# The first products of a hybrid decoder layer, issued kind by kind

## The chip, the cores and the metric

The kernel runs on one core of one Trainium2 chip. A time is device microseconds (us) for one execution of the whole layer. The profile is of one execution; its span goes from the first to the last instruction that the profiler saw.

Engines: PE (TensorE) multiplies matrices and has a weight-load stream of its own (PEld); DVE (VectorE) and ACT (ScalarE) do elementwise work; POOL (GpSimd) does little here; SP (SyncE) issues nearly all transfers. Each engine takes its instructions strictly in the order in which they were built; between engines they wait on semaphores.

## The reference, cut to what matters

```python
def hybrid_layer(x, norm1_w, w_in, ...):
    h = rmsnorm(x, norm1_w)
    proj = h @ w_in                       # ONE input projection, its columns split:
    qkv_a, z_a, b_a, a_a, qkv_b = ...     # gated DeltaNet (q, k, v, z, b, a) and attention
    qkv_a = silu(causal_dwconv(qkv_a, conv_qkv_w))
    ...                                   # L2-normed q and k, chunked delta rule, gated norm
    o_b = dilated_attention(qb, kb, vb)   # 3 dilated windows merged by their denominators
    x = x + concat([o_a, o_b]) @ w_out
    u = causal_dwconv(rmsnorm(x, norm2_w) @ w_up, ffn_conv_w)
    return x + (silu(gate) * up) @ w_down # and a final RMSNorm behind it
```

Sequence 1024, model width 1024, 4 DeltaNet heads of 128, 8 attention heads of 64, feed-forward width 2816, all float32.

## The kernel before, in words

Every large product is made of three. A float32 operand is split in a high part rounded to fp32r (`hi`) and the rest (`lo`); `mm3` (L204) adds w_hi·x_hi, w_hi·x_lo and w_lo·x_hi in one PSUM bank. The helper `split` (L210) makes `hi` with a copy on ACT and `lo` with a subtraction on DVE. `split_x` (L280) does the same for the input `xt`, times the norm's weight `n1`.

**The start.** The input comes as eight tiles `xt` of 128 rows (the contraction) by 1024 tokens, the weights of the keys of heads 0 to 2 as four tiles `wst` of two contraction tiles each (the loop over k at L300). Tile 0 comes in two halves of 512 tokens. `squares(k)` (L286) squares a tile on ACT and adds it to `acc` on DVE, for the RMSNorm, whose factor is applied only after the products. Meanwhile PE multiplies a tile of ones, `warm`, ten times (L355); a float32 product shows as two passes in the profile, so these are 20 rows.

**The first products.** `first` (L361) runs over the 8 contraction tiles; for each, over six PSUM banks `pst`, that is three heads times two halves of 512 tokens, with three products each: 144 products of 512 columns. The profile names them by what they read: `ps<-xhi,whi`, `ps<-xlo,whi`, `ps<-xhi,wlo`. A bank is complete with its last product at the eighth tile.

**What follows it.** `norms` (L380) slips small products in between: `ps<-xt,wba`, `ps<-acc,pick` (sums of squares), then `bat` and `rst` on DVE, a power on POOL, and two groups of four transposes of `rst` on PE, which DVE copies to `rstdB`. `gates` (L411) makes the decays `g` and their sums (`ps<-g,tri`). `first_keys` (L501) takes the six banks out: DVE multiplies each by `rstdB` (rows `xr<-ps,rstdB`), and `conv_silu` (L460) makes the keys `kT` of a head: one copy on ACT, three steps on DVE (`kT<-xr,gcw,kT` over 1023, 1022 and 1021 columns), a tanh on ACT (`xr<-kT`), a last step on DVE (`kT<-xr,kT`). `kprep` (L587) fills decay tiles `dec` on POOL with a select, exponentiates them on ACT, and transposes the keys on PE (`ps<-ident,kT`). `dense` (L508) then makes the other columns of the projection with 48 products each, in two banks that take turns with the first banks of `pst`.

**What sets the order.** Streams (`first`, `dense`, `norms`, `gates` and others) yield a time at which they may go on; `Weave` (L46) keeps a planned clock for PE and for each engine (`free`, `ready`) and lets the most urgent stream that is ready issue next. This fixes PE's order. DVE's and ACT's orders come from a scheduler that works on the finished program with a timeline of its own; `after` (L188) adds an order between two instructions without a wait.

Of the kernel before, what the change touches and what calls it, by code (L numbers as in the profile page):

```python
# [7 lines left out]
F32 = mybir.dt.float32  # L8
F32R = mybir.dt.float32r
AF = mybir.ActivationFunctionType  # L10
OP = mybir.AluOpType
# [4 lines left out]
P = 128  # L16
S = 1024
KT = 8
# [126 lines left out]
def hybrid_layer(tc, I, out):  # L145
    nc = tc.nc
    wv = Weave()
    ve = Engine(wv, nc.vector, "vector", 0.07, 0.00105)
    ac = Engine(wv, nc.scalar, "scalar", 0.12, 0.00085)

# [15 lines left out]
    def tile_(pool, shape, dt, name, tag, bufs):  # L166
        return wv.slot(pool.tile(list(shape), dt, name=name, tag=tag, bufs=bufs), tag, bufs)
# [3 lines left out]
    def A(name, tag, dt=F32, shape=(P, 1024)):  # L171
        if tag in TURNS:
            i = turns[tag] = turns.get(tag, -1) + 1
            tag = TURNS[tag][i % len(TURNS[tag])]
        return tile_(lp, shape, dt, name, tag, SLOTS[tag])

    def X(name, dt=F32R):
        return A(name, "X", dt)

    def const(name, shape, src=None):  # L180
        t = cp.tile(list(shape), F32, name=name)
        if src is not None:
            sy.dma_start(t, src)
        return t
# [3 lines left out]
    def after(inst, anchor, reason="keeps a slot free until it is needed"):  # L188
        tc.add_manual_dep(inst.ins, anchor.ins.name, order, reason=reason)

    def mm(dst, lhs, rhs, us, start=True, stop=True, **kw):
        tc.stamp_issue_order_token(nc.tensor.matmul(dst, lhs, rhs, start=start, stop=stop, **kw).ins, TOKEN)  # L192
        wv.product(us, dst, lhs, rhs)
# [10 lines left out]
    def mm3(dst, lhs, rhs, first, last, **kw):  # L204
        us = 0.2135 * rhs[0].shape[-1] / 512
        mm(dst, lhs[0], rhs[0], us, first, False, **kw)
        mm(dst, lhs[0], rhs[1], us, False, False, **kw)
        mm(dst, lhs[1], rhs[0], us, False, last, **kw)

    def split(src, hi, lo):  # L210
        ac.activation(hi, src, AF.Copy)
        return ve.tensor_tensor(lo, src, hi.bitcast(F32), op=OP.subtract)
# [19 lines left out]
    n1 = const("n1", [P, KT])  # L232
# [25 lines left out]
    def bank(tag, name="ps"):  # L258
        return tile_(pp_, (P, 512), F32, name, tag, 2)
# [7 lines left out]
    def half(i):  # L267
        return slice(i * 512, i * 512 + 512)
# [7 lines left out]
    xs, xts = [], []  # L276
# [3 lines left out]
    def split_x(xt, k, sl):  # L280
        hi, lo = xs[k]
        ac.activation(hi[:, sl], xt[:, sl], AF.Copy, scale=n1[:, k:k + 1])
        ve.scalar_tensor_tensor(lo[:, sl], xt[:, sl], n1[:, k:k + 1], hi[:, sl].bitcast(F32), op0=OP.mult,
                                op1=OP.subtract)

    def squares(k):  # L286

        sqs[k] = A("sq", "qa")
        ac.activation(sqs[k], xts[k], AF.Square)
        if k == 1:  # L290
            ve.tensor_tensor(acc, sqs[0], sqs[1], op=OP.add)
        elif k > 1:
            inst = ve.tensor_tensor(acc, acc, sqs[k], op=OP.add)
            if k == 6:
                after(inst, first_lo, "the products wait for these weights")
# [4 lines left out]
    for k in range(KT):  # L300
        if k == 4:

            sy.dma_start(wba[:, :, :8], I["wba"])
        xt = A("xt", ("kT*", "dv*")[k % 2])
        xts.append(xt)
        if k % 2 == 0:
            wst = tile_(wp, [P, 2, 384], F32, "wst", "wst", 2)
            whi, wlo = [A(nm, "uy", F32R, (P, 2, 384)) if k < 4 else A(nm, "kt", F32R, (P, 2, 384))
                        for nm in ("whi", "wlo")]
            wk0.append((whi, wlo))  # L310
        xs.append((X("xhi"), X("xlo")))
        if k == 0:
            sy.dma_start(wst[:, 0, :], I["w0"][0, :, 0])
            for h in range(2):
                sy.dma_start(xt[:, half(h)], I["xT"][:P, half(h)])
            sy.dma_start(wst[:, 1, :], I["w0"][0, :, 1])
            split(wst[:, 0, :], whi[:, 0, :], wlo[:, 0, :])
            for h in range(2):
                split_x(xt, 0, half(h))
            split(wst[:, 1, :], whi[:, 1, :], wlo[:, 1, :])  # L320
        else:
            if k % 2 == 0:
                sy.dma_start(wst, I["w0"][k // 2])
            parts = [half(0), half(1)] if k == 1 else [slice(0, S)]
            for sl in parts:
                sy.dma_start(xt[:, sl], I["xT"][k * P:(k + 1) * P, sl])
            if k % 2 == 0:
                wlast = split(wst, whi, wlo)
            for sl in parts:
                split_x(xt, k, sl)  # L330
            squares(k - 1)
        if k == 4:
            first_lo = wlast
        if k == 6:
            ve.tensor_tensor(wba[:, :, :8], wba[:, :, :8], n1[:, :, None].to_broadcast([P, KT, 8]), op=OP.mult)
    squares(KT - 1)


# [13 lines left out]
    ve.tensor_scalar(gw2, gnw, 0.5, None, op0=OP.mult)  # L352

    wbank = bank("atr", "warm")
    for _ in range(10):  # L355
        mm(wbank[:, :P], warm, warm, 0.3)


    pst = [bank(t) for t in ("hf", "asc", "ch") for _ in range(2)]

    def first():  # L361
        for k in range(KT):
            w = wk0[k // 2]
            for i in range(6) if k > 1 else (0, 2, 4, 1, 3, 5):
                yield wv.need(*xs[k], *w)
                m, h = divmod(i, 2)
                wm = [t[:, k % 2, m * P:(m + 1) * P] for t in w]
                mm3(pst[i], wm, [t[:, half(h)] for t in xs[k]], k == 0, k == KT - 1)
        wv.done.add("first")


# [1178 lines left out]
    def down(pd, i, op, sl, first, last_):  # L1550
        (whi, wlo), (hhi, hlo) = op
        c = slice(i * P, (i + 1) * P)
        mm3(pd[:, sl], (whi[:, c], wlo[:, c]), (hhi[:, sl], hlo[:, sl]), first, last_, skip_group_check=True)
# [229 lines left out]
```

## Time and profile before

| what | value |
|---|---|
| time, median of 3 runs | 1191.49 us (1191.37 to 1192.41) |
| time of the profiled execution | 1191.63 us |
| its span | 1189.8 us |
| PE busy | 1180.1 us, 99% of the span |
| DVE busy | 965.4 us, 81% |
| ACT busy | 573.2 us, 48% |
| POOL busy | 54.6 us, 5% |
| granted TensorE clock, mean | 0.998 |

A timeline row reads: start in us, length in us, engine, line of the kernel, operation, what it writes<-reads, shape, count; in brackets the engine's idle time before it and who ended it. Rows that follow each other with equal names are merged. The length of a matmul row holds its pipeline; the distance between two starts is what a product costs. Line 139 is the helper that records every DVE and ACT operation and line 192 is the one for products, so the names of the tiles tell what a row is.

### The profile page before, as it was taken

What the parts mean: (1) busy time and instruction counts of PE and PEld (TensorE: products, weight loads), DVE (VectorE), ACT (ScalarE), POOL (GpSimd) and SP (SyncE); (2) the same over time, 40 slices, a digit from 0 to 9 for tenths busy, and PEclk for the clock granted to TensorE, in tenths of its full rate; (3) what the DMA queues carried; (4) which work ended last, traced back from release to release, by engine and by line L of the source; (5) the groups of instructions that cost most, each with busy time, mean ns of one, the idle gap of its engine ahead of it and who ended that gap; (6) DMA issues with size and microseconds to landing.
All of it is one profiled execution on the core that took longest, in us unless ns stands there. A gap on an engine that the chain in (4) does not pass through costs nothing.

```text
span 1189.8 us, 18253 instructions
## 1 busy us (share of the span) xinstructions
PE 1180.1 (99%) x6994; PEld 975.9 (82%) x6994; DVE 965.4 (81%) x1545; ACT 573.2 (48%) x1122; POOL 54.6 (5%) x49
## 2 busy tenths in 40 slices
PE   9999999999999999999999999999999999999997
PEld 7888888888777777888888888888888888888887
DVE  7776996474677787677998898989889889898987
ACT  7473444363434444555554444545444553546452
POOL 0212001013000000000000000000000000000001
PEclk9999999999999999999999999999999999999999
DMA  7423457647552414343221313122231395356734
GB/s 239 107 94 84 114 144 163 201 149 186 166 147 72 99 37 151 142 159 107 89 92 68 107 53 107 57 103 81 80 102 58 120 377 202 124 178 220 239 98 160
DMA packets 114520, 156.91 MB, mean 132 GB/s; under 512 B 54368, under 2 KB 65408, under 8 KB 114432
## 3 DMA queue, kind: packets, MB, share of 16 engines
q1 hardware_dynamic: 113712, 155.21, 41.4%
q8 instruction: 55, 0.90, 0.3%
q10 hardware_dynamic: 720, 0.53, 0.1%
q14 instruction: 33, 0.27, 0.1%
HBM read 117.68 MB, written 38.03 MB: 131 GB/s over the span
## 4 chain that ended last, share of the span: by engine, by line
PE 97%; DVE 1%; ACT 0%; issue 0%; DVEq 0%; ACTq 0%
PE ps L192 47%; PE pa L192 20%; PE dw L192 18%; PE pc L192 10%; PE ps L201 1%; PE ps L196 1%; PE warm L192 0%; DVE x1h L139 0%; ACT sm L141 0%; DVE sm L141 0%; PE pd L192 0%; DVE avt L139 0%; DVE aqkv L139 0%; DVE wke L141 0%; DVE ct L141 0%
## 5 line engine op out<-in xcount | busy, mean ns | idle before, releaser
L192 PE MATMUL dw<-pr 128*128 128x512 f32 (+1 forms) x984 | 211.4, 376 | 0.0
L192 PEld LDWEIGHTS dw<-pr 128*128 128x128 f32 x984 | 176.7, 188 | 33.7
L192 PE MATMUL ps<-xhi,whi 128*128 128x512 f32 x448 | 183.7, 410 | 0.0
L192 PE MATMUL ps<-xhi,wlo 128*128 128x512 f32 x448 | 175.2, 391 | 0.0
L192 PE MATMUL ps<-xlo,whi 128*128 128x512 f32 x448 | 174.9, 391 | 0.0
L192 PE MATMUL pa<-T,pair 128*128 128x512 f32 x528 | 126.8, 389 | 0.0
L192 PEld LDWEIGHTS pa<-T,pair 128*128 128x128 f32 x528 | 99.1, 188 | 20.6
L192 PEld LDWEIGHTS ps<-xhi,whi 128*128 128x128 f32 x448 | 84.2, 188 | 18.9 <-issue 2.7
L192 PEld LDWEIGHTS ps<-xhi,wlo 128*128 128x128 f32 x448 | 84.1, 188 | 18.3
L192 PEld LDWEIGHTS ps<-xlo,whi 128*128 128x128 f32 x448 | 84.4, 188 | 14.9 <-DVE xlo L139 0.3
L139 ACT ACTIVATE u<-pa 128x512 f32<-128x512 f32 x44 | 26.4, 599 | 114.4 <-PE pa L192 114.4
L139 DVE SCALAR_TENSOR_TENSOR y<-xu,fcw,y 128x1023 f32<-128x1023 f32 (+1 forms) x44 | 56.4, 1281 | 22.1 <-ACT y L139 22.0
L139 ACT ACTIVATE pr<-wd 128x1024 fp32r<-128x1024 f32 x33 | 35.0, 1061 | 73.4 <-DVE wd L139 35.8
L192 PE MATMUL pa<-B,A 128*128 128x512 f32 x264 | 63.5, 389 | 0.0
L192 PE MATMUL pc<-B,pair 128*128 128x512 f32 x264 | 63.4, 389 | 0.0
L192 PE MATMUL pc<-T,S 128*128 128x512 f32 x264 | 63.4, 389 | 0.0
L192 PE MATMUL pa<-T,S 128*128 128x512 f32 x264 | 63.4, 389 | 0.0
L139 DVE TENSOR_TENSOR wst<-wst 128x512 f32<-128x512 f32 x88 | 60.4, 686 | 0.8
L139 ACT ACTIVATE whi<-wst 128x1024 fp32r<-128x1024 f32 (+2 forms) x38 | 38.5, 1013 | 46.5 <-PE ps L192 38.9
L192 PE MATMUL ps<-B,pair 128*128 128x512 f32 x252 | 60.5, 389 | 0.0
L141 ACT ACTIVATE sm<-sm,mx 128x128 f32<-128x128 f32 (+7 forms) x64 | 35.5, 556 | 49.7 <-DVE mx L141 49.7
L192 PEld LDWEIGHTS pa<-T,S 128*128 128x128 f32 x264 | 49.6, 188 | 10.3
(248 smaller groups left out, 2229.8 us busy)
## 6 DMA issues: line engine op xcount, KB each, us to landing
wst<-in_wu SPq DMA_DIRECT2D x44, 512.0 KB, 3.7
wd<-in_wd SPq DMA_DIRECT2D x44, 512.0 KB, 4.4
wst<-in_wi SPq DMA_DIRECT2D x25, 512.0 KB, 4.2
upark<-y SPq DMA_DIRECT2D x22, 512.0 KB, 3.6
r<-upark SPq DMA_DIRECT2D x22, 512.0 KB, 9.9
wa<-in_wd SPq DMA_DIRECT2D x22, 256.0 KB, 3.0
apark<-aqkv SPq DMA_DIRECT2D x8, 512.0 KB, 2.7
wst<-in_wo SPq DMA_DIRECT2D x8, 512.0 KB, 3.6
```

Of the source, the lines that this page charges most:

```text
L139: return getattr(eng, op)(*a, **kw)
L141: return getattr(eng, op)(*a, **kw)
L192: tc.stamp_issue_order_token(nc.tensor.matmul(dst, lhs, rhs, start=start, stop=stop, **kw).ins, TOKEN)
L196: tc.stamp_issue_order_token(nc.tensor.transpose(dst, src, ident).ins, TOKEN)
L201: tc.stamp_issue_order_token(nc.tensor.transpose(dst, src[rows], ident[rows, rows]).ins, TOKEN)
```

## The change

Five edits, all in the start of the kernel.

- `first` goes through a tile's products by kind. For the first two tiles three banks at a time (one half of the tokens): the three w_hi·x_hi, then the three w_hi·x_lo, then the three w_lo·x_hi. For the other six tiles all six banks: six products of a kind, then six of the next. The number of products is the same.
- The high part of the first half of tile 0 is made by two engines: ACT rounds its columns 0 to 255, DVE columns 256 to 511. The low part of the weights comes after the low part of this half on DVE.
- `squares(k)` is called two tiles later than its tile, not one.
- PE's leading products are 8, not 10.
- The planner's clocks of DVE and ACT begin at 1.1 us.

```diff
 def hybrid_layer(tc, I, out):
     nc = tc.nc
     wv = Weave()
+    wv.free.update(vector=1.1, scalar=1.1)
...
             sy.dma_start(wst[:, 1, :], I["w0"][0, :, 1])
-            split(wst[:, 0, :], whi[:, 0, :], wlo[:, 0, :])
-            for h in range(2):
-                split_x(xt, 0, half(h))
+            ac.activation(whi[:, 0, :], wst[:, 0, :], AF.Copy)
+            xhi, xlo = xs[0]
+            near, far = slice(0, 256), slice(256, 512)
+            ac.activation(xhi[:, near], xt[:, near], AF.Copy, scale=n1[:, :1])
+            ve.tensor_scalar(xhi[:, far], xt[:, far], n1[:, :1], None, op0=OP.mult)
+            lo = ve.scalar_tensor_tensor(xlo[:, half(0)], xt[:, half(0)], n1[:, :1], xhi[:, half(0)].bitcast(F32),
+                                         op0=OP.mult, op1=OP.subtract)
+            after(ve.tensor_tensor(wlo[:, 0, :], wst[:, 0, :], whi[:, 0, :].bitcast(F32), op=OP.subtract), lo)
+            split_x(xt, 0, half(1))
             split(wst[:, 1, :], whi[:, 1, :], wlo[:, 1, :])
...
-            squares(k - 1)
+            if k > 1:
+                squares(k - 2)
...
+    squares(KT - 2)
     squares(KT - 1)
...
-    for _ in range(10):
+    for _ in range(8):
         mm(wbank[:, :P], warm, warm, 0.3)
...
     def first():
         for k in range(KT):
             w = wk0[k // 2]
-            for i in range(6) if k > 1 else (0, 2, 4, 1, 3, 5):
-                yield wv.need(*xs[k], *w)
-                m, h = divmod(i, 2)
-                wm = [t[:, k % 2, m * P:(m + 1) * P] for t in w]
-                mm3(pst[i], wm, [t[:, half(h)] for t in xs[k]], k == 0, k == KT - 1)
+            for banks in ((0, 2, 4), (1, 3, 5)) if k < 2 else (range(6),):
+                for a, b in ((0, 0), (0, 1), (1, 0)):
+                    for i in banks:
+                        yield wv.need(*xs[k], *w)
+                        m, h = divmod(i, 2)
+                        mm(pst[i], w[a][:, k % 2, m * P:(m + 1) * P], xs[k][b][:, half(h)], 0.2135,
+                           k == a == b == 0, (k, a) == (KT - 1, 1))
         wv.done.add("first")
```

## The prediction

> **What bounds the kernel now.** I read the page first: busy time, then the chain that ended last; then all waits of PE (total, times, longest).
>
> ```profile
> PE 1180.1 (99%) x6994; PEld 975.9 (82%) x6994; DVE 965.4 (81%) x1545; ACT 573.2 (48%) x1122; POOL 54.6 (5%) x49
> PE 97%; DVE 1%; ACT 0%; issue 0%; DVEq 0%; ACTq 0%
> PE warm L192 <- DVE pick L139: 1.1, 1, 1.1
> PE ps L196 <- DVE rs L139: 0.7, 1, 0.7
> ```
>
> PE carries 97% of the chain, and its largest recorded waits are 1.1 and 0.7 us. So a microsecond counts only where it moves PE's own row: less work at the start, a hole closed, or a new hole. From the second group of dense products on, PE's built order is the same before and after; SP's and POOL's queues are the same throughout. What can change lies in the first 60 us, and a delay there is carried to the end, as PE has nothing to catch up with.
>
> Now the start, in order of time, all engines:
>
> ```profile
> 1.13 4.33 PE L192 MATMUL warm<-warm 128*128 128x128 f32 x20 [1.13 <-DVE pick L139]
> 4.71 0.76 PE L192 MATMUL warm<-warm 128*128 128x128 f32 x4
> 3.73 0.56 DVE L139 TENSOR_TENSOR wlo<-wst,whi 128x384 fp32r<-128x384 f32 x1 [2.47 <-ACT whi L139]
> 3.89 0.72 ACT L139 ACTIVATE xhi<-xt,n 128x512 fp32r<-128x512 f32 x1 [0.20 <-DMA xt<-in_xT]
> 4.65 0.75 DVE L139 SCALAR_TENSOR_TENSOR xlo<-xt,n,xhi 128x512 fp32r<-128x512 f32 x1 [0.36 <-ACT xhi L139]
> 5.22 0.48 PE L192 MATMUL ps<-xhi,whi 128*128 128x512 f32 x1
> 5.55 0.40 PE L192 MATMUL ps<-xlo,whi 128*128 128x512 f32 x1
> 9.44 0.39 PE L192 MATMUL ps<-xhi,whi 128*128 128x512 f32 x1
> 11.06 1.14 ACT L139 ACTIVATE xhi<-xt,n 128x1024 fp32r<-128x1024 f32 x1
> 12.47 1.28 DVE L139 SCALAR_TENSOR_TENSOR xlo<-xt,n,xhi 128x1024 fp32r<-128x1024 f32 x1
> 13.52 0.39 PE L192 MATMUL ps<-xhi,whi 128*128 128x512 f32 x1
> 13.80 0.50 PE L192 MATMUL ps<-xlo,whi 128*128 128x512 f32 x1
> 14.37 0.40 PE L192 MATMUL ps<-xhi,whi 128*128 128x512 f32 x1
> ```
>
> The reader is to see three things. Products 19 and 37 start at 9.44 and 13.52: 18 products in 4.08 us, 0.227 each. The 20 leading rows run to 5.22, although the first half's high part was done at 3.89 + 0.72 = 4.61. And PE slips twice on a low part: 0.33 from 5.22 to 5.55 (0.10 too many) and 0.85 for three products from 13.52 to 14.37 (0.17 too many; the tile's low part ended at 12.47 + 1.28 = 13.75).
>
> **Part 1, the start.** The row at 4.71 is the last four of twenty passes, so sixteen passes, which is eight products, end at 4.71. Those four took 5.22 − 4.71 = 0.51, or 0.13 each, while the sixteen took 3.58, or 0.22 each: PE ran at about half speed until some 5.0 us. High part of half 0: ACT's two rows give 0.42 us for 512 more columns, so 256 columns fewer is 0.21 less, 0.51 in all (estimate), ready at 4.40. DVE's half costs at most the 0.75 of the longer operation at 4.65, and lies in the 2.47 us that DVE was idle. Then the low part takes 0.75, to about 5.18, and the low weights 0.56, to 5.75. The first product starts at 4.71, half speed for 0.3 us, done by about 5.09; the second kind is wanted at 5.54 and is there; the third at 6.2 and is there. So product 19 starts at 5.09 + 17 × 0.227 = 8.95 in place of 9.44: 0.49 gained. At the third tile six products stand before the low part; they begin at 13.0 and reach it at 14.4, long behind 13.75: 0.17 more. Gain: 0.66 us. Bounds: nothing, if half speed lasts 1.3 us longer; and 0.51 + 0.10 + 0.17 = 0.78, were nothing slow.
>
> The calls of `squares` cost nothing and bring nothing: the squares stand at the same places in ACT's built order as before. The planner's two clocks have no row of their own; what they bring is the order that I use.
>
> **Part 2, the norm's chain.** In DVE's built order a second low weight now stands ahead of `bat`.
>
> ```profile
> 29.72 0.44 DVE L141 STREAM_TRANSPOSE bat<-ps 128x256 f32<-128x256 f32 x1
> 30.79 1.23 DVE L139 TENSOR_TENSOR wlo<-wst,whi 128x1024 fp32r<-128x1024 f32 x1 [0.63 <-ACT whi L139]
> 31.93 0.16 DVE L141 TENSOR_SCALAR rst<-bat 128x8 f32<-128x8 f32 x1
> 36.63 0.19 DVE L139 SCALAR_TENSOR_TENSOR g<-az,ea 128x32 f32<-128x32 f32 x1
> 37.80 0.31 PE L192 MATMUL ps<-g,tri 128*128 128x32 f32 x2
> ```
>
> `bat` moves behind 30.79 + 1.14 = 31.93, `rst` to 32.4: the chain to `g` is 0.44 later and ends at 37.26. PE wants `g` at 37.80 − 0.66 + 0.45 (two more products stand ahead of it) = 37.59. Cost 0, margin 0.3; without that cover up to 0.4.
>
> **Part 3, the banks and the first keys.** This is the price. By triples, bank 0 was complete with the third product of the last tile; by kind its last product is the thirteenth there, ten products later. DVE's order follows: all six evictions, then the keys' steps; before, five, a step, the sixth.
>
> ```profile
> 40.77 0.40 PE L192 MATMUL ps<-xhi,wlo 128*128 128x512 f32 x1
> 43.07 0.39 PE L192 MATMUL ps<-xhi,whi 128*128 128x512 f32 x1
> 41.21 3.43 DVE L139 TENSOR_TENSOR xr<-ps,rstdB 128x512 f32<-128x512 f32 x5
> 44.56 1.27 DVE L139 SCALAR_TENSOR_TENSOR kT<-xr,gcw,kT 128x1023 f32<-128x1023 f32 x1
> 45.75 0.68 DVE L139 TENSOR_TENSOR xr<-ps,rstdB 128x512 f32<-128x512 f32 x1
> 46.35 6.81 DVE L139 SCALAR_TENSOR_TENSOR kT<-xr,gcw,kT 128x1023 f32<-128x1023 f32 x4
> 53.09 0.68 DVE L139 TENSOR_TENSOR xr<-ps,rstdB 128x512 f32<-128x512 f32 x1
> 53.26 1.06 ACT L139 ACTIVATE xr<-kT 128x1024 f32<-128x1024 f32 x1 [5.63 <-DVE kT L139]
> 54.35 1.22 DVE L139 SCALAR_TENSOR_TENSOR kT<-xr,kT 128x1024 f32<-128x1024 f32 x1 [0.58 <-ACT xr L139]
> 56.68 1.03 PE L196 MATMUL ps<-ident,kT 128*128 128x128 f32 x8
> 45.74 1.10 POOL L139 TENSOR_SCALAR_AFFINE_SELECT dec<-dec 128x1024 f32<-128x1024 f32 x1 [11.92 <-DMA dec<-gdram]
> 48.16 5.95 POOL L139 TENSOR_SCALAR_AFFINE_SELECT dec<-dec 128x1024 f32<-128x1024 f32 x3 [1.32 <-DMA dec<-gdram]
> ```
>
> Before, bank 0's last product (40.77) ended at 41.17 and its eviction began at 41.21. The product that now completes bank 0 stands at the place of the row at 43.07; 0.66 earlier it starts at 42.41, ends at 42.80, and the eviction begins at 42.84: 1.63 later than before, in spite of the gain. Then DVE, by steps from one start to the next: an eviction 0.60 (45.75 to 46.35), a key step 1.19 (44.56 to 45.75). Six evictions: 46.44. In the new order four key steps, an eviction and a fifth key step lie ahead of head 0's tanh: 5 × 1.19 + 0.60 = 6.55, to 52.99.
>
> POOL's selects come on top. The four key steps from 46.35 to 53.09 took 6.74, not 4 × 1.19 = 4.76: 1.98 more, in the stretch in which POOL made its four selects, and POOL's three from 48.16 took 5.95, not 3 × 1.10. Single eviction rows beside them kept their 0.68. I take the same 1.98: head 0's steps end at 54.97. From the last step to the tanh it was 53.26 − 53.09 = 0.17; the tanh 1.06 and 0.03 to hand over (54.35 less 54.32): 56.23; last step 1.22: 57.45; PE starts about 0.05 behind (13.75 to 13.80): 57.50. Before, the keys were done at 55.57 and PE came to them at 56.68, with 1.1 us to spare. Now PE arrives at 56.68 − 0.66 = 56.02 and waits 1.48. Nothing can pass it: PE is in order, and the dense products are queued behind these transposes. Net: 57.50 − 56.68 = 0.82 us later than before.
>
> Bounds of the collisions: with none, the keys are done at 55.47, PE does not wait, and the whole gain of 0.66 stays. At most, each select pushes DVE as far as DVE pushed POOL's three, which took 5.95 − 3.30 = 2.65 more; four of them make 3.53 in place of 1.98: the keys 1.55 later, net 2.4 us. I take 1.98, the row that is nearest: the same steps beside the same selects.
>
> [...]
>
> What is late next: head 1's keys. They were done at 61.6 (60.37 + 1.22) for transposes at 65.05; in the new order a low weight, a step of head 3, a step of its own and an eviction come ahead of its last step.
>
> ```profile
> 60.37 1.22 DVE L139 SCALAR_TENSOR_TENSOR kT<-xr,kT 128x1024 f32<-128x1024 f32 x1
> 63.75 1.11 DVE L139 TENSOR_TENSOR aqkv<-ps,rstdB 128x512 f32<-128x512 f32 x1
> 65.05 0.60 PE L196 MATMUL ps<-ident,kT 128*128 128x128 f32 x4
> ```
>
> From 57.45: 1.19 + 1.23 + 1.19 + 1.19 + 1.11, then tanh and last step with 2.3, is 65.7 at the latest; PE comes at 65.05 + 0.82 = 65.87. Cost 0, margin 0.2; if it goes, it costs tenths.
>
> **Sum.** −0.66 (start) + 1.48 (wait for head 0's keys) = +0.82 on the profiled execution's 1191.63, which lies 0.14 above the median of the runs; span and what lies around it (1.83) move together. On the median of 1191.49: 1192.3 us. That is 0.07%. About 0.2% (2.4 us) is what a measurement of this kernel can tell from no change.
>
> **The rivals.**
> Keys in time: the selects fall beside the evictions, which do not collide, and the start's gain stays: 1191.49 − 0.66 = 1190.8. For it: the evictions now fill 42.8 to 46.4, where the first select lies. Against it: the other three begin at 48.16, when DVE is in its key steps under either order.
> Keys very late, the case on the slow side: the same wait on DVE, but the selects cost 3.5 and head 1 misses its margin, so that each group of transposes waits. It decides from a wait of 3.1 us for head 0's keys: +2.4 and more; with 0.4 for head 1, 1194.3. For it: margins of 0.2 and 0.3 only. Against it: before, one of the steps in that stretch cost nothing extra.
> Slow start: with two leading products fewer, full speed comes one stretch later. The 16 slow passes lasted 3.6; one more such stretch at half speed loses 1.8, the banks are later by as much, and so are the keys: 0.82 + 1.8 = 2.6, 1194.1. Against it: the row at 4.71 shows the change of speed before the first product, and PE has no idle time before it in either version. [...]
> Small change of another kind, either sign, inside 1 us: any of the other margins.
>
> **How the numbers follow.** Forecast 0.50; keys in time 0.20; keys very late 0.12; slow start 0.06; other small change 0.08; large gain from a cause that I do not see 0.04. Within 0.2%: 0.50 + 0.20 + 0.08 = 0.78. Slower: 0.18. Faster: 0.04. Range: from 1190.6 (keys in time, with the 0.78) to 1194.3 (both slow cases' centres), about 2 in 10 outside.
>
> **What would show it.** The first product at about 4.7 and the fourth, now `ps<-xlo,whi`, without a hole; product 37 at 12.9; the first `xr` eviction near 42.8; a wait of PE for DVE `kT` of about 1.5 us, the transposes near 57.5; from there all of PE 0.8 later than before. Wrong if PE shows no wait there, if the key steps between 46.4 and 55 take their bare 1.19 each, if the slow passes reach beyond 5.1 us, or if PE's rows behind 66 us shift against each other.

## The result and the profile after

| | runs | median | lowest to highest |
|---|---|---|---|
| kernel before | 22 | 1192.05 us | 1191.37 to 1193.23 |
| changed kernel | 22 | 1193.57 us | 1192.55 to 1195.96 |

The ratio is 1.0015, with a 95% interval of 1.0009 to 1.0020; the medians differ by 1.5 us. So the change costs time, though less than the 0.2% that I called no change. The time lies inside the range, 1.3 us above the forecast of 1192.3. Of these, 0.6 are the kernel before, whose median is 1192.05 over these 22 runs and was 1191.49 over the three to which I added; as a difference, 0.82 was forecast and 1.52 came. The profiled execution of the changed kernel took 1194.73 us, its span 1192.9 us; the mean granted clock was 0.997.

First the page and the waits of PE in the changed kernel (total, times, longest), which answer to the first fence of the prediction. Line numbers are one or more higher than before (193 for 192, 197 for 196).

```profile
PE 1181.0 (99%) x6990; PEld 976.4 (82%) x6990; DVE 965.6 (81%) x1546; ACT 572.8 (48%) x1122; POOL 55.8 (5%) x49
PE 96%; DVE 2%; ACT 1%; issue 0%; DVEq 0%; ACTq 0%
PE ps L197 <- DVE kT L139: 2.1, 1, 2.1
```

One wait is new and is now the largest: PE stands for DVE's `kT`, 2.05 us. DVE's share of the chain has gone from 1 to 2%. The start, by the timeline of the changed kernel:

```profile
3.89 0.51 ACT L139 ACTIVATE xhi<-xt,n 128x256 fp32r<-128x256 f32 x1 [0.27 <-DMA xt<-in_xT]
4.43 0.75 DVE L139 SCALAR_TENSOR_TENSOR xlo<-xt,n,xhi 128x512 fp32r<-128x512 f32 x1 [0.17 <-ACT xhi L139]
4.45 0.98 PE L193 MATMUL ps<-xhi,whi 128*128 128x512 f32 x3
5.27 0.94 PE L193 MATMUL ps<-xlo,whi 128*128 128x512 f32 x3
8.78 0.84 PE L193 MATMUL ps<-xhi,whi 128*128 128x512 f32 x3
```

The first product starts at 4.45 instead of 5.22, and product 19 at 8.78 instead of 9.44. The low part, which used to open a hole behind the first product, is wanted at 5.27 and is there. Then the norm's chain, the evictions and the keys, all engines:

```profile
36.96 0.19 DVE L139 SCALAR_TENSOR_TENSOR g<-az,ea 128x32 f32<-128x32 f32 x1
37.40 0.31 PE L193 MATMUL ps<-g,tri 128*128 128x32 f32 x2
42.63 3.68 DVE L139 TENSOR_TENSOR xr<-ps,rstdB 128x512 f32<-128x512 f32 x6 [1.93 <-PE ps L193]
46.23 7.36 DVE L139 SCALAR_TENSOR_TENSOR kT<-xr,gcw,kT 128x1023 f32<-128x1023 f32 x4
53.51 0.68 DVE L139 TENSOR_TENSOR xr<-ps,rstdB 128x512 f32<-128x512 f32 x1
54.11 1.50 DVE L139 SCALAR_TENSOR_TENSOR kT<-xr,gcw,kT 128x1021 f32<-128x1021 f32 x1
55.53 0.68 DVE L139 TENSOR_TENSOR xr<-ps,rstdB 128x512 f32<-128x512 f32 x1
56.80 1.23 DVE L139 SCALAR_TENSOR_TENSOR kT<-xr,kT 128x1024 f32<-128x1024 f32 x1 [0.58 <-ACT xr L139]
46.16 1.10 POOL L139 TENSOR_SCALAR_AFFINE_SELECT dec<-dec 128x1024 f32<-128x1024 f32 x1 [12.25 <-DMA dec<-gdram]
48.43 6.10 POOL L139 TENSOR_SCALAR_AFFINE_SELECT dec<-dec 128x1024 f32<-128x1024 f32 x3 [1.17 <-DMA dec<-gdram]
58.07 1.35 PE L197 MATMUL ps<-ident,kT 128*128 128x128 f32 x8 [2.05 <-DVE kT L139]
```

The six evictions stand together, as forecast, and the first starts at 42.63 (41.21 before). Head 0's keys are done at 58.03 and PE starts their transposes at 58.07, 1.4 us later than before, though it had arrived at 56.02. What comes next on PE was not in any of my cases:

```profile
59.08 0.78 PE L193 MATMUL ps<-xhi,whi 128*128 128x512 f32 x1
59.65 0.63 PE L193 MATMUL ps<-xlo,whi 128*128 128x512 f32 x1
60.08 0.63 PE L193 MATMUL ps<-xhi,wlo 128*128 128x512 f32 x1
...
62.20 0.39 PE L193 MATMUL ps<-xlo,whi 128*128 128x512 f32 x1
62.44 0.40 PE L193 MATMUL ps<-xhi,wlo 128*128 128x512 f32 x1
```

From 59.65 to 62.20 the products come every 0.43 us, not every 0.227, and then at the usual pace again. This is half speed: the granted clock was 0.50 from 58.77 to 62.18. It makes the profiled execution another 1.65 us later, 3.05 in all, and that stays to the end.

### The profile page after: what moved, and what is told of

Same layout as the page of the kernel before. It is cut to its first block, busy times and chain, and to the rows that moved or that the text cites. A ratio compares the mean times of both kernels' runs of the same rounds, so it can differ in the third digit from the quotient of the medians.

```text
span 1192.9 us, 18245 instructions
## 1 busy us (share of the span) xinstructions
PE 1181.0 (99%) x6990; PEld 976.4 (82%) x6990; DVE 965.6 (81%) x1546; ACT 572.8 (48%) x1122; POOL 55.8 (5%) x49
## 4 chain that ended last, share of the span: by engine, by line
PE 96%; DVE 2%; ACT 1%; issue 0%; DVEq 0%; ACTq 0%
PE ps L193 46%; PE pa L193 20%; PE dw L193 17%; PE pc L193 10%; PE ps L197 1%; PE ps L202 1%; DVE kT L139 1%; DVE xr L139 0%; DVE x1h L139 0%; ACT sm L141 0%; PE warm L193 0%; DVE sm L141 0%; PE pd L193 0%; DVE avt L139 0%; DVE aqkv L139 0%
## 5 line engine op out<-in xcount | busy, mean ns | idle before, releaser
L193 PE MATMUL ps<-xhi,whi 128*128 128x512 f32 x448 | 178.4, 412 | 0.0
L193 PE MATMUL ps<-xhi,wlo 128*128 128x512 f32 x448 | 170.2, 393 | 0.0
L193 PE MATMUL ps<-xlo,whi 128*128 128x512 f32 x448 | 169.6, 392 | 0.0
L193 PEld LDWEIGHTS pc<-B,pair 128*128 128x128 f32 x264 | 49.6, 188 | 10.3
```

## The experiments

**Theory.** The start gains a few tenths. The last tile by kind completes bank 0 ten products later, so DVE makes head 0's keys late, PE waits for them in order, and behind that wait its clock falls to half. **Rivals.** The loss lies in the leading products, in the norm's chain or in the planner's orders; or in the keys of all heads, so that a wait taken away at head 0 comes back; and half speed may have nothing to do with the wait. The times of the experiments stand beside runs of the kernel before on the same chip in the same session; 0.0010 in a ratio is 1.2 us.

### Only the last tile bank by bank

```diff
-            for banks in ((0, 2, 4), (1, 3, 5)) if k < 2 else (range(6),):
+            for banks in ((0, 2, 4), (1, 3, 5)) if k < 2 else (range(6),) if k < KT - 1 else [(i,) for i in range(6)]:
```

> The changed kernel, but the last of the eight tiles goes bank by bank again; everything else of the change stays. Theory (bank 0 is complete ten products later, so the keys are late): the first eviction starts at 40.7 to 41.0 instead of 42.63, the keys of head 0 are done by about 55.6, PE comes to their transposes at about 55.7 and waits 0.3 us or less instead of 2.05, its clock stays full behind them, and the gain of the start is kept: 1192.05 - 0.95 = 1191.1 us. Rival (the loss lies in the leading products, the norm's chain or the planner's orders, and the hole only shows it): PE still waits over 1 us near the transposes and the time stays near 1193.5.

Measured: 1191.68 us (11 runs) against 1192.45 (28 runs); ratio 0.9994, interval 0.9985 to 1.0003. Its timeline:

```profile
6.86 0.72 ACT L139 ACTIVATE xhi<-xt,n 128x512 fp32r<-128x512 f32 x1 [2.40 <-DMA xt<-in_xT]
7.63 0.96 PE L193 MATMUL ps<-xhi,whi 128*128 128x512 f32 x3 [0.70 <-ACT xhi L139]
41.97 3.18 DVE L139 TENSOR_TENSOR xr<-ps,rstdB 128x512 f32<-128x512 f32 x5
55.41 1.23 DVE L139 SCALAR_TENSOR_TENSOR kT<-xr,kT 128x1024 f32<-128x1024 f32 x1 [0.59 <-ACT xr L139]
57.18 1.03 PE L197 MATMUL ps<-ident,kT 128*128 128x128 f32 x8
```

The wait is gone: keys done at 56.64, PE there at 57.18 with no idle time ahead of the row. So one loop header undoes the whole loss and leaves a kernel that lies, by the medians, some 0.8 us below the one before. My absolute times missed by a microsecond, and the first two rows say why: in this execution the second half of tile 0 landed late (`xhi` at 6.86; 5.59 in the changed kernel's profile), and PE, which now comes to it sooner, waited 0.70 for it. The start's gain depends on that landing.

### The order by kind alone

The kernel before with the changed loop of `first`, and nothing else of the change.

```diff
-            for i in range(6) if k > 1 else (0, 2, 4, 1, 3, 5):
-                yield wv.need(*xs[k], *w)
-                ...
-                mm3(pst[i], wm, [t[:, half(h)] for t in xs[k]], k == 0, k == KT - 1)
+            for banks in ((0, 2, 4), (1, 3, 5)) if k < 2 else (range(6),):
+                for a, b in ((0, 0), (0, 1), (1, 0)):
+                    for i in banks:
+                        ...
```

> The kernel before, but its first products go by kind as in the change; ten leading products, the first half on one engine, squares and planner's clocks as before. Theory: no gain at the start, and the last tile's order makes the keys late by itself: first eviction at about 43.5, keys of head 0 done at about 58.8, a wait of PE of about 2.2 us, and with half clock behind it or without 1194.2 to 1196. Rival (the loss comes from the other edits): no wait over 0.5 us, 1192 us.

Measured: 1194.82 us (11 runs) against 1192.45; ratio 1.0019, interval 1.0011 to 1.0028.

```profile
43.45 3.68 DVE L139 TENSOR_TENSOR xr<-ps,rstdB 128x512 f32<-128x512 f32 x6 [3.29 <-PE ps L192]
57.38 1.23 DVE L139 SCALAR_TENSOR_TENSOR kT<-xr,kT 128x1024 f32<-128x1024 f32 x1 [0.58 <-ACT xr L139]
58.66 1.09 PE L196 MATMUL ps<-ident,kT 128*128 128x128 f32 x8 [1.81 <-DVE kT L139]
```

The order alone costs 2.4 us by the medians. Without the start's gain that is more than the whole change, though the two intervals overlap. The eviction, the keys and the time came where they were expected; the wait was 1.81, not 2.2. The second profile of the kernel before, below, happened to have full speed from the same moment (5.40 and 5.41 us): there the transposes start at 56.62, so this pair differs by 2.04 us at the transposes, and by 2.05 us in the time of the executions (1194.00 and 1191.95).

### How much of the last tile by kind

Two kernels that stand between: only the first two tiles by kind, all others bank by bank; and the last tile by kind over two banks at a time.

```diff
-            for banks in ((0, 2, 4), (1, 3, 5)) if k < 2 else (range(6),):
+            for banks in ((0, 2, 4), (1, 3, 5)) if k < 2 else [(i,) for i in range(6)]:
```

> The changed kernel, but only the first two tiles go by kind (three banks at a time); the six tiles behind them go bank by bank as before the change. Theory: the gain of the change lies in these two tiles and the start, its loss in the last tile alone, so this is the variant with only the last tile by bank once more: no wait at head 0's transposes, no half speed, 0.6 to 0.9 us below the kernel before. Rival (the six tiles by kind bring part of the gain): 0.3 us or more slower than the variant with only the last tile by bank, which lay 0.77 below.

```diff
-            for banks in ((0, 2, 4), (1, 3, 5)) if k < 2 else (range(6),):
+            for banks in ((0, 2, 4), (1, 3, 5)) if k < 2 else (range(6),) if k < KT - 1 else ((0, 1), (2, 3), (4, 5)):
```

> The changed kernel, but the last tile goes by kind over two banks at a time, so that bank 0 is complete with the fifth product of that tile (bank by bank: the third; by kind over six banks: the thirteenth). Theory (the loss follows the place of that product, 0.227 us each, and DVE's order behind it): DVE makes four evictions, a key step and two evictions; the keys of head 0 are done about 0.5 us later than bank by bank, PE waits at most 0.5 us, and the time lies 0 to 0.4 us above the variant bank by bank. Rival (any order by kind in the last tile costs the same): a wait of 1.5 us or more and 1 us above the kernel before.

Measured: 1191.85 us (ratio 0.9994, interval 0.9985 to 1.0003) and 1191.82 us (0.9996, 0.9987 to 1.0005), 11 runs each, against 1192.38 (21 runs). The timeline of the second:

```profile
41.09 2.67 DVE L139 TENSOR_TENSOR xr<-ps,rstdB 128x512 f32<-128x512 f32 x4
54.62 1.22 DVE L139 SCALAR_TENSOR_TENSOR kT<-xr,kT 128x1024 f32<-128x1024 f32 x1 [0.59 <-ACT xr L139]
56.11 1.04 PE L197 MATMUL ps<-ident,kT 128*128 128x128 f32 x8
```

Neither waits for the keys. With bank 0 complete at the fifth product of the last tile in place of the thirteenth, keys done at 55.84 are in time for a PE that comes at 56.11. Three kernels that close bank 0 early thus lie 0.5 to 0.8 us below the kernel before; each interval still holds "no change", and the three can't be told from each other, so neither the theory's nor the rival's 0.3 us for the six middle tiles is settled.

### POOL's selects left out

```diff
-        po_.affine_select(v8(dec), v8(dec), pattern=[[0, NCH], [1, P]], compare_op=OP.is_ge, fill=NEG,
-                                base=0, channel_multiplier=-1)
+        wv.account("gpsimd", 0.15 + 0.0021 * 1024, [dec], [dec], 0.28)
...
-            inst = ac.activation(v8(dec)[:, c, :], v8(dec)[:, c, :], AF.Exp, bias=ngc[:, c, h:h + 1])
+            inst = ac.activation(v8(dec)[:, c, :], v8(dec)[:, c, :], AF.Exp, scale=0.0, bias=floor)
```

> The changed kernel without POOL's four selects on the decays (the exponentials then read a constant bias at scale 0, so the decays of the heads are left out of the result); the orders of PE and DVE are the same. Theory (the selects stretch the key steps): the four steps from 46.2 take about 4.8 us instead of 7.4, the step at 54 takes its bare 1.2, head 0's keys are done at about 55.4, PE waits under 0.3 us, time about 1191.1. Rival (the steps are stretched by something else, such as PE's or ACT's traffic): the steps still take over 7 us and the wait stays about 2 us.

Measured: 1192.49 us (10 runs) against 1192.45; ratio 1.0000, interval 0.9991 to 1.0009. This kernel leaves the decays out of its result, so only its times say something.

```profile
47.70 4.85 DVE L139 SCALAR_TENSOR_TENSOR kT<-xr,gcw,kT 128x1023 f32<-128x1023 f32 x4
53.08 1.27 DVE L139 SCALAR_TENSOR_TENSOR kT<-xr,gcw,kT 128x1021 f32<-128x1021 f32 x1
56.15 0.69 DVE L139 TENSOR_TENSOR xr<-ps,rstdB 128x512 f32<-128x512 f32 x1 [1.80 <-PE ps L193]
56.76 1.22 DVE L139 SCALAR_TENSOR_TENSOR kT<-xr,kT 128x1024 f32<-128x1024 f32 x1
58.03 1.09 PE L197 MATMUL ps<-ident,kT 128*128 128x128 f32 x8 [0.56 <-DVE kT L139]
```

Without the selects the four steps take 4.85 us in place of 7.36, and the fifth 1.27 in place of 1.50: the selects, not traffic of PE or ACT, stretch the key steps, by 2.7 us in all. Step by step, the four start 1.19 or 1.20 us apart here. In the changed kernel they start at 46.23, 48.26, 49.45 and 51.48 and the eviction behind them at 53.51: three of the four took 2.03 us, which is 0.84 more, and one took its bare 1.19. Taking the selects out is worth 1.5 us of the time, each kernel against its own runs of before (+0.04 and +1.52). But 1191.1 did not come, and 0.56 of the wait stays. The row at 56.15 shows what I had missed: an eviction of a dense bank stands in DVE's order ahead of head 0's last key step, and DVE itself waits 1.80 us there for PE to complete that bank. However fast the key steps are, the keys can't be done before that bank is out, and PE comes to the transposes just before. Two engines in order, each behind the other, left half a microsecond here.

### The transposes later in PE's order

```diff
-        yield wv.need(kT, slack=SLACK + 1.5 * (h == 0))
+        yield wv.need(kT, slack=SLACK + 3.5 * (h == 0))
```

> The changed kernel with PE's built order moved at one place: the transposes of head 0's keys come nine dense products later (the planner's slack for head 0 raised by 2 us). Theory (the loss is PE standing in order behind late keys): PE comes to the transposes about 2.05 us later, just when the keys are done, so the wait there is 0 to 0.4 us, no half speed follows, and the time is 0.3 us or less above the variant that closes its last tile by bank: some 0.5 us below the kernel before. Rival (the heads' chain as a whole is late, and the wait comes back at the later heads): the waits behind head 0's transposes grow by 1 us and more in sum, and the time stays 1 us and more above the kernel before.

Measured: 1195.02 us (11 runs) against 1192.39 (26 runs); ratio 1.0022, interval 1.0012 to 1.0031.

```profile
58.96 1.03 PE L197 MATMUL ps<-ident,kT 128*128 128x128 f32 x8
65.75 1.23 DVE L139 SCALAR_TENSOR_TENSOR kT<-xr,kT 128x1024 f32<-128x1024 f32 x1 [1.09 <-ACT xr L139]
67.04 0.66 PE L197 MATMUL ps<-ident,kT 128*128 128x128 f32 x4 [1.59 <-DVE kT L139]
```

```profile
PE ps L193 <- ACT sq L141: 0.9, 1, 0.9
```

My theory fell here and the rival held (the last line is from the waits of PE). The nine dense products fill the wait for head 0. But PE then comes sooner to head 1's transposes, whose keys on DVE come no sooner: 1.59 us there, and 0.88 more at 85.3 us. Together they make 2.5 us, about the loss (2.6 us by the medians). Here, putting other work ahead of a wait did not help, as the next operand came from the same late engine. The small margin that the prediction gave head 1 was real.

### The wait and half speed

Eight products of the identity with itself in the wait, then a second profile of the changed kernel, then a longer wait.

```diff
             pt = yield from next_bank("atr", src)
+            if hh == 0 and src is T["k", 0]:
+                for _ in range(8):
+                    tc.stamp_issue_order_token(nc.tensor.matmul(pt[:, :P], ident, ident).ins, TOKEN)
```

> The changed kernel, with eight products of the identity with itself (16 passes of 128 columns, about 1.8 us, into the bank that the transposes then overwrite) on PE ahead of the transposes of head 0's keys. Theory (the clock falls to half because PE stood idle there): the transposes start where they did, 58.0 to 58.1, the products behind them keep 0.227 us each, the clock records show no half speed behind 10 us, and all executions lie near 1193.2, none at a mean clock of 0.997. Rival (half speed has another cause, such as the transposes or what DVE does then): the half-speed stretch of 3.4 us stays in about half of the executions, and the median stays at 1193.6.

Measured: 1196.24 us (6 runs) against 1192.45; ratio 1.0032, interval 1.0020 to 1.0044.

```profile
PE ps L193 <- issue: 0.9, 1, 0.9
56.98 1.95 PE L585 MATMUL ps<-ident 128*128 128x128 f32 x16
58.77 1.04 PE L197 MATMUL ps<-ident,kT 128*128 128x128 f32 x8
59.56 0.48 PE L193 MATMUL ps<-xhi,whi 128*128 128x512 f32 x1
```

No half speed followed the filled gap (full speed held for 1181.011 us from 7.00), but the experiment is spoilt as a measure of time: the 16 passes ran past the keys (done at 58.31) by 0.46 us, and PE later stood 0.9 us at "issue", near 206 us, a stall that the other kernels don't have and that I can't explain. The expected 1193.2 did not come. Nor did the expected mean clock: four of the six executions had 0.996 or 0.997, so half speed probably came in executions of which there is no profile. Since the next profile shows that the changed kernel too can go without half speed, this experiment decides nothing.

The changed kernel, unedited, profiled a second time:

> The changed kernel itself, one more look. Theory (speed is decided window by window of 3.413 us, counted from the moment full speed begins, and only a window that was idle for more than half is followed by half speed): the clock records of the first look have boundaries at 55.36 and 58.77, and 2.05 us of the 3.41 between them were idle; in this look full speed begins elsewhere between 4.2 and 7.6 us, and half speed follows only if about 2 us of the wait fall in one window; if a boundary cuts the wait in two, the products behind the transposes keep 0.227 us. Rival (any wait of 2 us is followed by half speed): half speed again, whatever the boundaries.

Measured: 1193.41 us. The windows view cuts the span at the boundaries that the clock records give (us from and to, length; busy time of PE, PEld, DVE, ACT, POOL; granted clock; two figures on transfers). First the changed kernel's first profile, whose full speed began at 4.16, then this one, 5.49.

```profile
55.36:58.77 3.41, 1.36 (x9) 0.89 (x9) 2.83 (x5) 3.06 (x4) 0.00 (x0) 1.00 0.01 2
58.77:62.18 3.41, 3.41 (x11) 2.76 (x10) 3.41 (x5) 3.41 (x15) 0.00 (x0) 0.50 0.26 55
```

```profile
53.27:56.69 3.42, 3.18 (x14) 2.26 (x13) 3.37 (x4) 0.56 (x1) 1.70 (x1) 1.00 0.00 0
56.69:60.10 3.41, 1.60 (x11) 1.50 (x12) 2.88 (x4) 3.41 (x7) 0.00 (x0) 1.00 0.01 2
60.10:63.51 3.41, 3.41 (x16) 2.80 (x15) 3.22 (x4) 3.41 (x17) 0.00 (x0) 1.00 0.47 111
```

The wait is the same, 2.05 us. In the first profile all of it lies in one window: PE idle 3.41 − 1.36 = 2.05, 60%, and the next window runs at 0.50. In the second a boundary cuts it: 0.24 and 1.81 (53%), and the clock stays at 1.00. The boundaries fit: 4.158 + 16 × 3.413 = 58.77.

```diff
+        if j == 4:
+            nc.vector.scalar_tensor_tensor(y, xr, 0.0, y, op0=OP.mult, op1=OP.add)
         th = ac.activation(xr, y, AF.Tanh, scale=0.5)
```

> The changed kernel with one more DVE step on head 0's keys ahead of the tanh (it adds zero times the input; 1.2 us). PE's order is equal. Theory (PE waits for the keys, step for step; and a speed window of 3.413 us that was idle for more than about 55% is followed by half speed): the wait is 3.1 to 3.3 us; unless a boundary cuts it near its middle, one window holds 2 us or more of it, and half speed for 3.41 us follows from the end of that window; the time is 1.2 us (no half speed in either) to 2.9 us above the changed kernel. Rival (half speed has nothing to do with the wait): at most as often as before, here too without regard to the boundaries; the time is 1.2 us above.

Measured: 1197.19 us (4 runs) against 1192.38; ratio 1.0036, interval 1.0022 to 1.0050. Full speed from 6.49; the windows:

```profile
57.69:61.10 3.41, 0.77 (x7) 0.77 (x8) 3.41 (x5) 2.62 (x5) 0.00 (x0) 1.00 0.25 48
61.10:64.52 3.42, 3.42 (x11) 2.74 (x10) 2.92 (x4) 3.42 (x15) 0.00 (x0) 0.50 0.27 108
```

The wait was 3.44 us (3.1 to 3.3 expected), 2.64 of it (77%) in one window, and half speed came exactly with the next boundary, 0.77 us behind the first transposes and not at the end of the wait. The waits of 1.81 in the order alone (56.85 to 58.66) and in the first variant of the next section (57.64 to 59.45) each lie whole in one window, by the clock records 56.61 to 60.02 and 57.21 to 60.63, and no half speed followed. So the rival is out: half speed follows a window, and for this pattern the dividing line lies between 53 and 60% idle, with idle time counted from the ends that the profile gives the rows. The time is 2.5 us above the changed kernel's by the ratios (1.0036 and 1.0015), between the 1.2 and 2.9 expected.

### The other edits

Squares one tile later and the planner's clocks at zero; then ten leading products; each in the changed kernel.

```diff
-    wv.free.update(vector=1.1, scalar=1.1)
...
-            if k > 1:
-                squares(k - 2)
+            squares(k - 1)
...
-    squares(KT - 2)
```

> The changed kernel with the squares one tile later and the planner's clocks at zero, as before the change; the order by kind, the two-engine first half and eight leading products stay. DVE then has `bat` between the two low weights again. Theory (these two edits cost and bring nothing): PE starts `g,tri` without a wait as in the changed kernel, the first eviction and the keys of head 0 stand where they stood within 0.2 us against PE's products, the wait is about 2 us, the time that of the changed kernel within 0.3 us. Rival (the norm's chain or the planner's order makes the keys late): wait below 1 us, time 1 us and more lower.

Measured: 1194.20 us (10 runs) against 1192.39; ratio 1.0017, interval 1.0008 to 1.0026. The timeline around `g`:

```profile
37.27 0.19 DVE L139 SCALAR_TENSOR_TENSOR g<-az,ea 128x32 f32<-128x32 f32 x1
37.56 0.38 PE L192 MATMUL ps<-g,tri 128*128 128x32 f32 x2 [0.69 <-PE ps L196]
```

The time is that of the changed kernel as far as the intervals tell, and the wait for the keys is 1.81. But one expectation failed: with the old settings PE comes to `g,tri` 0.69 us too early (the row names the transposes ahead of it, but `g` ended at 37.46). In the changed kernel PE has no such wait. So the two edits are worth up to 0.7 us together with the order by kind; which of them was not tried.

```diff
-    for _ in range(8):
+    for _ in range(10):
```

> The changed kernel with ten leading products as before the change; all other orders are equal. Theory (the two leading products are plain time ahead of the first product): the first product starts 0.4 to 0.6 us later than the 4.45 to 4.57 us of eight, the keys and PE move together, so the wait at the transposes stays 1.5 to 2.1 us, and the time is 0.3 to 0.5 us above the changed kernel. Rival (fewer leading products delay full speed): full speed comes earlier with ten, product 19 is not later, and the time is equal or lower.

Measured: 1194.47 us (11 runs) against 1192.39; ratio 1.0018, interval 1.0009 to 1.0028. The first product started at 5.42, 0.85 later than the 4.57 of most profiles with eight, more than expected, as all four passes ran at half speed; the wait was 1.24, less than expected, as two of the four key steps took 2.03 us in this execution and not three (6.52 us for the four). The time stands 0.03% above the changed kernel's ratio, which the intervals don't resolve; the rival's earlier full speed did not come (6.38 us).

The kernel before, unedited, profiled a second time:

> The kernel before itself, one more look. In eight looks at kernels with the start of the change, full speed began anywhere between 4.16 and 7.00 us; in the one look at the kernel before it began at 5.02. Theory (that moment is a matter of the execution, not of the kernel, so the looks at the start differ by it): where it comes later than about 5.5 us here, the first product starts near 5.4 to 5.6, the products up to that moment take 0.43 us each, and product 19 starts later than 9.44 by about 0.47 us for each microsecond of delay. Rival (ten leading products bring full speed at a fixed place, about 5.0): product 19 at 9.4 to 9.5 again.

Measured: 1191.95 us. Full speed came at 5.40, so the theory's condition of 5.5 was just missed; product 19 started at 9.58, 0.14 later than in the first profile, not at 9.4 to 9.5. One table of all the profiles says it better (us; read from the rows and clock records of each trace):

| kernel | full speed from | first product | product 19 | `xhi` of tile 0's second half begins |
|---|---|---|---|---|
| before, first and second profile | 5.02; 5.40 | 5.22; 5.41 | 9.44; 9.58 | 5.38; 5.76 |
| order by kind alone | 5.41 | 5.42 | 9.61 | 5.69 |
| changed, first and second profile | 4.16; 5.49 | 4.45; 4.57 | 8.78; 9.21 | 5.59; 5.58 |
| last tile by two banks | 4.39 | 4.48 | 8.79 | 5.59 |
| last tile bank by bank | 4.26 | 4.52 | 9.91 | 6.86 |
| only the first two tiles by kind | 5.44 | 4.57 | 9.63 | 6.58 |
| no selects | 6.56 | 4.57 | 9.99 | 6.93 |
| wait filled | 7.00 | 4.57 | 9.90 | 5.64 |
| squares and clocks as before | 6.01 | 4.57 | 9.45 | 5.79 |
| longer wait | 6.49 | 4.57 | 9.68 | 6.13 |
| ten leading products | 6.38 | 5.42 | 10.06 | 5.62 |
| transposes later | 6.93 | 4.57 | 9.87 | 5.79 |

Full speed comes anywhere from 4.16 to 7.00 with eight leading products and from 5.02 to 6.38 with ten, and the landing of the second half moves by 1.5 us. Between them they spread product 19 over 8.78 to 9.99 in the kernels with the start of the change, which is more than the change gains there. At nearly equal moments of full speed the change brings 0.37 (9.58 to 9.21), and two leading products 0.38 (10.06 to 9.68).

## Why the prediction was right, point by point

A loss too small to call a change, and the range, were right; the loss itself was 0.82 in the forecast and 1.52 by the medians. The wait behind late keys was the right mechanism, and its size was put too low. By the steps of the prediction:

- **Part 1, the start: right in kind, the size hangs on the execution.** Forecast 0.66, with 0.78 as the upper bound. Between the first profiles it is 0.66 at product 19 (0.49 forecast there; full speed came 0.86 us earlier in the one) and 0.86 some 26 us into the span (the 140th row behind the leading passes, 26.37 and 25.51), which is above the bound. Between the second profiles, with nearly equal full speed, it is 0.37 and 0.36, and half speed lasts until 5.49, beyond the 5.1 that I had named as a sign of being wrong. The hole at the third tile was no fixed loss: the second profile of the kernel before ran from product 37 to that row in 12.65 us, 0.20 less than the first. The three variants that keep the start and close bank 0 early lie 0.5 to 0.8 below the kernel before by their medians, so 0.66 was a fair size. What I had treated as fixed rows, the moment of full speed and the landing of the second half, came out otherwise in each execution (5.02 and 5.40, and `xhi` at 5.38 and 5.76, in the two profiles of the kernel before).
- **Part 2, the norm's chain: right.** `g` ended at 37.15 (37.26 forecast) and PE took it at 37.40 without a wait. The margin belonged to the order with the planner's clocks and the squares as changed; with the old ones there is none.
- **Part 1's sentence on squares and clocks** ("cost nothing and bring nothing") was too strong: they are up to 0.7 us, in the order that I used.
- **Part 3, banks: right.** First eviction 42.63 (42.84 forecast), six evictions to 46.23 (46.44).
- **Part 3, the selects: mis-sized.** I took 1.98 us from the row of before. From 46.23 the four key steps took 53.51 − 46.23 = 7.28, 2.52 more than 4 × 1.19, and the fifth 0.23 more: 2.75 in place of 1.98. The first select began at 46.16, right ahead of the first key step; before, it had begun at 45.74 beside an eviction. My upper bound, 3.53, holds it. The run without selects confirms the cause and the bare steps (4.85 for four). The price has a plain form that I could have read off the profile of before: a step that meets a whole select takes 2.03 in place of 1.19, so 0.84 more. There the 1.98 were two such steps (starting at 49.03 and 51.06) and 0.30 at 46.35; now they were three and the 0.23 of the fifth. So the term failed in the count of meetings and not in the cause. The stretched steps and the three selects from 48.43 both come 2.0 apart: in the changed kernel the steps at 49.45 and 51.48 take 2.03 each, the three selects 6.10 together.
- **Part 3, the keys and the wait:** done at 58.03 (57.45 forecast) and a wait of 2.05 (1.48). The 0.58 are the selects' 0.77, less the 0.21 by which the evictions came earlier. PE's arrival at 56.02 was forecast to the hundredth, by luck: the start gained 0.86 and not 0.66, and a wait is counted from the end of the last product's row, not from where the next row would have started. That product started at 55.63 and its row ends at 56.02, 0.39 behind; before, the transposes started 0.23 behind the last product. So 0.16 more is lost than the wait shows; with 0.04 in the rows ahead of it, it makes the 0.2 by which the way from the 140th row to the transposes is longer (30.51 and 30.31 us).
- **The missing step: half speed behind the wait.** No term and no rival had it. My slow start had the clock at the wrong end: I asked what the clock does before the first product and not what a hole of 2 us does to it in the middle. It cost 1.65 us in the first profile, where one window held the wait, and nothing in the second, where a boundary cut it. How often either happens two profiles don't tell, but the mean granted clock of each execution does in part. It is 0.997 in the two profiles of this case that have a halved window behind a wait and 0.998 in the twelve that have none. Of the 22 executions of the changed kernel 14 have 0.998, and their median is 1193.38, still 1.3 above the kernel before. So most of the medians' 1.5 us stands without half speed. (0.997 proves nothing by itself: 10 of 28 executions of the kernel before have it too.)
- **Nothing else shifts behind 66 us: right** within 0.5 us: from 66 us to the end the distance between the changed kernel and the one before goes from 3.06 to 3.01 in the first profiles and from 1.97 to 1.46 in the second.
- **The rivals.** Keys in time: out, by the selects and, without them, by the eviction in DVE's order. Keys very late: no, the wait was below 3.1 and head 1 held its margin; moving the transposes used it up. Slow start: full speed came between 4.16 and 7.00 with eight leading products and between 5.02 and 6.38 with ten, so no stretch more is to be seen, and with ten the time was no lower.

So the sum for two executions with nearly equal full speed (the second profiles of both kernels) reads −0.37 + 2.05 + 0.20 = 1.88, which is what the transposes show (58.50 against 56.62); their times differ by 1.46, and the medians by 1.52. The forecast had −0.66 + 1.48 = 0.82.

## What to carry to other kernels

When products of one accumulation are reordered, ask when each bank is complete, not only when each operand is wanted: here the changed start brought 0.37 us at nearly equal full speed, and going by kind, with a consumer that waits for the first bank of the last tile, cost more than that (2.4 us by the medians, in the order alone). Price a new hole on PE twice, once as the wait (2.05 us here) and once as a stretch of half speed that may follow it (1.65 us in one profile, nothing in the other). And before tenths are read out of two profiles, set their executions side by side where they have the same start.

## What the runs showed of the hardware that I had not expected

In these profiles speed changed by windows of 3.413 us, whose grid lay differently in each execution (full speed from 4.16 and from 5.49 in the two of the changed kernel). In twelve profiles full speed lasted 1181.011 us from its beginning, 346 such windows; in the two others it was cut after 54.613 us, 16 windows; the half speed behind it lasted 3413 ns in the clock records of the changed kernel's first profile. (The last 3.7 to 5.8 us of every span are at half speed too, at a granted clock of 0.50, which is why the mean clock is 0.998 and not 1.) The first profile of the changed kernel, the longer wait and the cases without half speed agree with one reading: idle 1.81 us of a window (53%) left the next one at full speed, 2.05 (60%) and 2.64 (77%) halved it. So 40% of a window at work did not save the next one from half speed. The work in those windows was transposes and products; whether the two count alike no run shows, so the dividing line is one for this pattern.

In the table above, the moment of first full speed, 4.16 to 7.00 us with PE at work from 1.13, spreads over 2.8 us, which is most of one window. Windows ahead of the first clock record are shown with a clock of 1.00 in the windows view; there the rows' own lengths have to be read (in the first profile of the kernel before, passes 0.21 us apart up to 4.92 and 0.11 from 5.08 on; the prediction's 0.13 mixes the two).

DVE's key steps and POOL's selects stretched each other here, the steps at a nearly fixed price: in every profile with selects two or three of the four steps from the end of the evictions took 2.02 to 2.04 us in place of 1.19. How many meet a select differs between executions: the same four steps took 7.36, 7.00, 6.52 us in profiles of kernels with equal orders, and 4.85 without the selects. The three selects from 48.43 took 6.10 us in the changed kernel's first profile; the first one, from 46.16, took 1.10.
